# A two-layer GLA and S5 trunk: GpSimd's elementwise work goes to VectorE

## The chip, the cores and the metric

The kernel runs on one core of a Trainium2 chip. Its time is the device time of one execution in microseconds; the figure used is the median of three runs. Engines are TensorE (PE in the profile, its weight loads PEld), VectorE (DVE), ScalarE (ACT), GpSimd (POOL) and SyncE (SP, which here only issues DMAs).

## The reference

512 tokens of width 1024 pass two layers, each `x <- x + Mixer(RMSNorm(x))`, and a last RMSNorm. The first mixer is chunked gated linear attention (GLA) with 4 heads; the second is a grouped complex-diagonal state-space layer (S5) with 128 groups of 16 channels and 64 states each:

```
lam_bar = exp(lam * dt);  b_bar = (lam_bar - 1) / lam * b
states  = scan(states * lam_bar + b_bar u)
y = Re(c states) + d u;   y = gelu(y);   y = y * sigmoid(y w_glu + b_glu) * silu(z)
```

Everything is float32. All inputs arrive at run time, the S5 parameters too, so the matrices with which the S5 layer is computed are made in the kernel.

## The kernel before

**Dense products.** Every weight matrix comes in units of 128x1024 floats. `wunit` (L178) loads a unit into `wraw` (two buffers), lets ScalarE round it to a high half (`whl`, L161) and makes the low half, raw minus high, with `split` (L159, the subtraction is L162). `three` (L196) then does three matmuls per product. With `dma=True` (w_v of heads 1 to 3, w_z, w_qk) the low half is made by a DMA instead: ScalarE writes minus the raw unit (L186) and a DMA from GpSimd's queue adds the raw unit (L187). With `pool=True` (the S5 projections u and z and the first block of w_glu, 40 units) a list of zeros and ones, `UNITP`, says whether GpSimd or VectorE subtracts; 23 units go to GpSimd.

**The GLA layer** runs head by head. `weave` (L544) steps through the dense generators of a head and calls between the steps the parts of its attention (`scores`, `state`, `mix`) and, through `hook` (L369), the next steps of the S5 preparation, at a rate per phase (`RATES`).

**The S5 preparation** (class `S5Prep`). `small` (L971) makes the parameter tables, in good part on GpSimd (L993). Then for each of 16 blocks of 8 groups: `load` (L1271) fetches four tiles, `compute` (L1285) makes the products L1293 to L1311 on GpSimd, step F of the next block adds z and z2 on VectorE (`finish_b`, L1323) and stores the input matrix in two halves (`store`, L1317 on ScalarE, L1318 on VectorE), and step Z (`finish_z`, L1326) stores the output matrix, multiplies it with bh on TensorE (L1333) and makes from that the direct kernel (L1337 on ScalarE, L1339 on VectorE, L1342 to L1345 on GpSimd) and stores it. Step E (`etab`, L1250) makes one of eight tables of rotations with six products, on VectorE for the first `EV = 3` and on GpSimd for the others. Results go to DRAM and are fetched back by the S5 layer.

**The S5 layer.** For each block: `sT` transposes u, `sA` (L795) multiplies it with the input matrix, rotates, scans (L810), and rotates back: L812 on GpSimd, L813 to L815 on VectorE. `sB` (L817) makes halves of the state (L822, L823) and the output; `sC` the gelu; `s5` (L843) the product with the gate (L847, GpSimd) and the halves for the GLU.

**Order.** Each engine runs its instructions in one order, which a planner fixes ahead from priorities. `LOWS` puts the steps F, Z, E and G so far behind the work around them in priority. Each engine's queue, SyncE's DMA queue too, is worked through in that order. GpSimd also issues the adding DMAs (L187) and makes the powers of the RMS norms (L270).

Of the kernel before, what the change touches and what calls it, by code (L numbers as in the profile page):

```python
# [21 lines left out]
P = 128  # L22
# [33 lines left out]
TS = [2, 3, 3, 3, 4, 5, 5, 5, 6, 6, 7, 8, 10, 10, 11, 12]  # L56
ORDER = ['u0', 'u1', 'u2', 'z0', 'u3', 'z1', 'z2', 'z3', 'g0']
LOW1, LOW2 = 20, 0
EV = 3
SCP = -20  # L60
USP = 50
SEQ0 = 'h0 u h2 u h4 u s h6 u x0 t x1 q0 q1 t'
GP = 4
RATES = [0.84, 0.84, 0.88, 0.94, 0.94]
LOWS = {'F': 0, 'Z': 20, 'E': 100, 'G': 0}
ETABS = [2, 3, 3, 3, 3, 3, 3, 3, 4, 4, 4, 4, 4, 4, 4, 7, 8]
POS = [[0, 0, 1, 2, 1, 2, 3, 1, 2, 3, 3], [0, 1, 1, 3, 4, 5, 6, 5, 5, 7, 9], [0, 1, 3, 4, 4, 5, 6, 5, 6, 8, 8], [1,
    1, 4, 4, 4, 5, 6, 6, 6, 6, 8], [0, 0, 0, 0]]
# [5 lines left out]
SGS = [16, 16, 16, 16, 16, 16, 16, 16, 16, 16, 16, 17, 18, 19, 20, 21]  # L74
LAS = [0, 0, 0, 5, 6, 7, 8, 9, 10, 10, 11, 12, 13, 14, 15, 16]
LBS = [0, 0, 0, 6, 7, 7, 8, 9, 10, 11, 12, 13, 14, 15, 16, 18]
UNITP = [0, 1, 0, 1, 1, 1, 0, 1, 1, 1, 0, 1, 1, 0, 1, 1, 1, 1, 1, 0, 0, 1, 1, 1, 1, 1, 0, 1, 0, 0, 1, 0, 0, 0, 0, 0,
    0, 0, 1, 1]
TORD = ['c0 c1 s0 c2 x0 s1 x1 c3 s2 x2 x3', 'c0 c1 c2 c3 x0 s0 s1 x1 s2 x2 x3', 'c0 c1 c2 c3 s0 x0 s1 s2 x1 x2 x3',
    'c0 c1 c2 c3 s0 s1 x0 x1 s2 x2 x3']  # L80
PACE = [2, 2, 2, 2, 2, 2, 3, 1, 2, 2, 2, 2, 2, 2, 2, 2, 2, 2, 1, 1, 1, 1]
# [4 lines left out]
def f(t):  # L86
    return t.bitcast(F32) if t.dtype == F32R else t
# [3 lines left out]
def trunk_kernel(  # L91
# [5 lines left out]
    nc = tc.nc  # L97
# [58 lines left out]

    mark = {}

    def split(dst_hi, dst_lo, src, scale=None, E=V):  # L159
        if scale is None:  # L160
            i0 = A.copy(out=dst_hi, in_=src)  # L161
            i1 = E.tensor_tensor(out=dst_lo, in0=src, in1=f(dst_hi), op=SUB)  # L162
        else:
            i0 = A.activation(out=dst_hi, in_=src, func=AF.Copy, scale=scale)
            i1 = V.scalar_tensor_tensor(out=dst_lo, in0=src, scalar=scale, in1=f(dst_hi), op0=MUL, op1=SUB)  # L165
        return i0.ins, i1.ins
# [6 lines left out]
            V.tensor_scalar(out=dst_hi, in0=src, scalar1=scale, scalar2=None, op0=MUL)  # L173
            V.scalar_tensor_tensor(out=dst_lo, in0=src, scalar=scale, in1=f(dst_hi), op0=MUL, op1=SUB)

    wcnt = [0]

    def wunit(src, nk, ncol, pool=False, dma=False):  # L178
        raw = T_([P, nk, ncol], "wraw", WR)
        mark["sp"] = S.dma_start(out=raw.rearrange("p k n -> p (k n)"), in_=src).ins  # L180
        hi = T_([P, nk, ncol], "whl", WH, F32R)
        lo = T_([P, nk, ncol], "whl", WH, F32R)
        if dma:
            fl = "p k n -> p (k n)"
            A.copy(out=hi, in_=raw)  # L185
            mark["act"] = A.activation(out=lo, in_=raw, func=AF.Copy, scale=-1.0).ins  # L186
            G.dma_start(out=lo.rearrange(fl), in_=src, accum_op=ADD)  # L187
        else:
            E = V
            if pool:  # L190
                E = G if UNITP[wcnt[0]] else V
                wcnt[0] += 1
            mark["act"], mark["dve"] = split(hi, lo, raw, E=E)
        return hi, lo

    def three(acc, wh, wl, ah, al, first, last, weights_stationary):  # L196
# [6 lines left out]
            PE.matmul(acc, lhsT=ah, rhs=wl, start=False, stop=False)  # L203
            mark["pe"] = PE.matmul(acc, lhsT=al, rhs=wh, start=False, stop=last).ins  # L204

    def dense_tok(w, ah, al, evac, per_tb=False, late=True, major=1, pool=False, banks=None, dma=False):
        nkb = 4 if per_tb else len(ah)
        accs = [b() for b in banks or [PD] * NT]
        nu = nkb // 2

        def part(u, tb, hi, lo):
            for k in range(2):
                kb = 2 * u + k
                if per_tb:
                    cs = slice(kb * P, (kb + 1) * P)
                    xh, xl = ah[tb][:, cs], al[tb][:, cs]
                else:
                    cs = slice(tb * P, (tb + 1) * P)
                    xh, xl = ah[kb][:, cs], al[kb][:, cs]
                three(accs[tb], hi[:, k, :], lo[:, k, :], xh, xl, kb == 0, kb == nkb - 1, False)  # L220

        def fetch(u):
            return wunit(w[u], 2, 512, pool=pool, dma=dma)
        for u in range(nu - major + 1):
            if u == nu - major:
                ws = [fetch(v) for v in range(u, nu)]
                for tb in range(NT):
                    for i, (hi, lo) in enumerate(ws):
                        part(u + i, tb, hi, lo)
                    if major > 1:  # L230
                        evac(tb, accs[tb])
                if major > 1:
                    yield
                    return
            else:
                hi, lo = fetch(u)
                for tb in range(NT):
                    part(u, tb, hi, lo)
            if u == nkb // 2 - 1:
                if late:  # L240
                    yield
                for tb in range(NT):
                    evac(tb, accs[tb])
            if not (late and u == nkb // 2 - 1):
                yield

    def dense_ch(w, ah, al, evac, pool=False, banks=None):
        nkb = len(ah)
        accs = [b() for b in banks or [PD] * 4]
        for u in range(nkb // 2):  # L250
            hi, lo = wunit(w[u], 2, 512, pool)
            for m in range(4):
                for k in range(2):
                    kb = 2 * u + k
                    three(accs[m], hi[:, k, m * P:(m + 1) * P], lo[:, k, m * P:(m + 1) * P],
                          ah[kb], al[kb], kb == 0, kb == nkb - 1, True)
            if u == nkb // 2 - 1:
                for m in range(4):
                    evac(m, accs[m])
            yield  # L260
# [494 lines left out]
    def ev_z(cb, acc):  # L755
        zt = tmp()
        V.tensor_tensor(out=zt, in0=acc, in1=rb2, op=MUL)
        th = tmp()
        A.activation(out=th, in_=zt, func=AF.Tanh, scale=0.5)
        if cb < 12:  # L760
            z = big()
        else:
            if not z3:
                z3.append(T_([P, 4, 512], "u8", 1))
            z = z3[0][:, cb - 12]
        sz[cb] = z
        V.scalar_tensor_tensor(out=z, in0=th, scalar=1.0, in1=zt, op0=ADD, op1=MUL)
# [27 lines left out]
    def sA(cb):  # L795
        t = st_[cb]
        bm, uh = t["bm"], t["uh"]
        co, sn = t["cs"]
        r = rz[cb % 2]
        pv = PO()  # L800
        for g in range(GB):
            three16(pv, bm, g, uh[:, 0], uh[:, 1], True, True)
        t2 = tmp()
        V.tensor_tensor(out=t2[0:64], in0=pv[64:128, :], in1=sn[64:128, :], op=MUL)
        V.scalar_tensor_tensor(out=t2[64:128], in0=pv[0:64, :], scalar=-1.0, in1=sn[0:64, :], op0=MUL, op1=MUL)
        t1 = t["t1"] = tmp()
        V.tensor_tensor(out=t1, in0=pv, in1=co, op=MUL)
        V.tensor_tensor(out=t1, in0=t1, in1=t2, op=ADD)
        sh = xx()
        V.tensor_tensor_scan(out=sh, data0=r.rearrange("p g c -> p (g c)"), data1=t1, initial=0.0,  # L810
                             op0=MUL, op1=ADD)
        G.tensor_tensor(out=t1, in0=sh, in1=co, op=MUL)  # L812
        V.scalar_tensor_tensor(out=t2[0:64], in0=sh[64:128], scalar=-1.0, in1=sn[64:128], op0=MUL, op1=MUL)  # L813
        V.tensor_tensor(out=t2[64:128], in0=sh[0:64], in1=sn[0:64], op=MUL)
        V.tensor_tensor(out=t1, in0=t1, in1=t2, op=ADD)  # L815
# [27 lines left out]
    def s5(cb):  # L843
        if yh2[cb // 8] is None:
            yh2[cb // 8] = act2()
        yh[cb] = yh2[cb // 8][:, cb % 8, :]
        G.tensor_tensor(out=sz[cb], in0=sz[cb], in1=yv[cb], op=MUL)  # L847
        yl[cb] = xx(F32R) if cb == 0 else big(F32R)
        split(yh[cb], yl[cb], yv[cb])
        yv[cb] = None  # L850
# [12 lines left out]
    def win():  # L863
        for c in ORDER:
            n = int(c[1])
            if c[0] == "u":
                yield from dense_tok(s_wu[n], h2, l2, lambda tb, acc, n=n: ev_u(n, tb, acc), late=False, pool=True)
            elif c[0] == "z":
                yield from dense_ch(s_wz[n], h2, l2, lambda m, acc, n=n: ev_z(4 * n + m, acc), pool=True)
            else:  # L870
                yield from dense_ch(w_glu[n], yh, yl, lambda m, acc, n=n: ev_g(4 * n + m, acc), pool=True)

    jobs = {}

# [64 lines left out]
class S5Prep:  # L939
# [309 lines left out]

    def etab(self, ck):  # L1250
        nc = self.nc
        tt = (nc.vector if ck < EV else nc.gpsimd).tensor_tensor
        gs = slice(ck * GB, (ck + 1) * GB)
        hr, hi, lr, li = (t[:, gs] for t in self.et)
        shp = [P, GB, 8, 8]
# [27 lines left out]
        self.ld[cb] = (lp, bb, xc, pp)  # L1283

    def compute(self, cb):  # L1285
        G = self.nc.gpsimd
        tt = G.tensor_tensor
        lp, bb, xc, pp = self.ld.pop(cb)
        gs = slice(cb * GB, (cb + 1) * GB)
        v = lambda t: t.rearrange("p (g r q) -> p g r q", g=GB, r=2)  # L1290
# [35 lines left out]
    def finish_z(self, cb):  # L1326
# [10 lines left out]
        A.activation(out=ke, in_=pk[:, 0:P], func=AF.Copy, scale=self.par[:, 0:1])  # L1337
        kf = self.C2([P, P, 2], "kf", F16)
        V.scalar_tensor_tensor(out=ke, in0=pk[:, P:2 * P], scalar=self.par[:, 1:2], in1=ke, op0=MUL, op1=ADD)  # L1339
        G = nc.gpsimd  # L1340
        dk = self.C2([P, 16], "dk")
        G.tensor_tensor(out=dk, in0=self.dm, in1=self.kd[:, cb:cb + 1].to_broadcast([P, 16]), op=MUL)  # L1342
        G.tensor_tensor(out=ke[:, 0:16], in0=ke[:, 0:16], in1=dk, op=ADD)
        G.tensor_copy(out=kf[:, :, 0], in_=ke)
        G.tensor_tensor(out=kf[:, :, 1], in0=ke, in1=kf[:, :, 0], op=SUB)  # L1345
        S.dma_start(out=self.kz[cb * GB:(cb + 1) * GB, :, 224:480].rearrange("g i w -> (g i) w"),
                    in_=kf.rearrange("p w k -> p (w k)"))

# [81 lines left out]
```

## Time and profile before

| | us |
|---|---|
| three runs | 1053.78, 1055.71, 1055.98 |
| median | 1055.71 |
| the profiled execution | 1054.56 |
| its span in the profile | 1052.9 |

| engine | busy us | share of the span |
|---|---|---|
| PE | 927.6 | 88% |
| DVE | 713.8 | 68% |
| POOL | 511.0 | 49% |
| ACT | 472.2 | 45% |

A busy time is the time in which at least one instruction of that engine was under way; it includes time in which the instruction stood still. The rows that the prediction rests on stand below. In groups of instructions, a row gives line, engine, operation, output<-inputs, shapes and count, then busy time and mean length, then the idle time before them and what ended it.

### The profile page before, as it was taken

To read this page: it belongs to the slowest core of one execution; us is meant where nothing else is said; L and a number is where in the kernel's file an instruction comes from. 1 tells how busy PE (TensorE), PEld (TensorE's weight loads), DVE (VectorE), ACT (ScalarE), POOL (GpSimd) and SP (SyncE) were. 2 spreads that over 40 slices of the span, in tenths; PEclk is the share of its full clock that TensorE was granted. 3 is DMA by queue.
4 is the path that set the end of the run, shared out by engine and by line. 5 is a ranking of instruction groups with operands and counts; after the bars stand their busy time and mean duration, and the time that the engine had idled before them with its cause. 6 is when DMAs were issued, how large, how long until landed. Compare 5 with 4: busy or idle time off the path is not lost. (4 is left out here: it accounts for less than half of the span.)

```text
span 1052.9 us, 13715 instructions
## 1 busy us (share of the span) xinstructions
PE 927.6 (88%) x5019; PEld 720.8 (68%) x5019; DVE 713.8 (68%) x916; ACT 472.2 (45%) x707; POOL 511.0 (49%) x477
## 2 busy tenths in 40 slices
PE   6795966699869796969989999999998999999996
PEld 5573754457646684747777777787777888888885
DVE  5794569957898887978645769789897432424322
ACT  5553343445546455433556684744453332313222
POOL 4164808976897979899973434453314000000000
PEclk9897987999889998989999999999999999999998
DMA  8884466999969899999578447687854323353312
GB/s 256 221 183 100 87 167 185 276 247 262 265 209 250 228 292 273 237 321 317 190 226 259 151 121 250 211 300 252 264 185 140 110 82 99 100 160 100 100 61 80
DMA packets 118707, 205.79 MB, mean 195 GB/s; under 512 B 32400, under 2 KB 69824, under 8 KB 118640
## 3 DMA queue, kind: packets, MB, share of 16 engines
q1 hardware_dynamic: 110208, 180.90, 55.2%
q0 software_dynamic: 5472, 19.02, 10.0%
q10 hardware_dynamic: 2960, 4.99, 1.3%
q8 instruction: 39, 0.64, 0.3%
q14 instruction: 28, 0.23, 0.1%
HBM read 167.69 MB, written 45.59 MB: 203 GB/s over the span
## 5 line engine op out<-in xcount | busy, mean ns | idle before, releaser
L162 DVE TENSOR_TENSOR whl<-wraw,whl 128x1024 fp32r<-128x1024 f32 x77 | 106.6, 1384 | 147.5 <-ACT whl L161 147.3
L161 ACT CAST whl<-wraw 128x1024 fp32r<-128x1024 f32 x100 | 104.7, 1048 | 183.7 <-PE pt L199 46.0
L202 PE MATMUL pd<-whl,actA 128*128 128x512 f32 x384 | 154.6, 408 | 12.9 <-ACT whl L161 9.2
L203 PE MATMUL pd<-whl,actA 128*128 128x512 f32 x384 | 154.2, 402 | 0.0
L204 PE MATMUL pd<-whl,actA 128*128 128x512 f32 x384 | 154.0, 404 | 0.0
L270 POOL TENSOR_TENSOR rstd<-rv,neghalf 128x1 f32<-128x1 f32 (+1 forms) x6 | 5.2, 874 | 248.4 <-DVE rv L269 248.4
L198 PE MATMUL pd<-actA,whl 128*128 128x512 f32 x256 | 101.6, 403 | 3.3 <-ACT u L732 3.1
L200 PE MATMUL pd<-actA,whl 128*128 128x512 f32 x256 | 101.4, 397 | 0.0
L202 PEld LDWEIGHTS pd<-whl,actA 128*128 128x128 f32 x384 | 74.4, 194 | 32.7 <-ACT whl L161 9.2
L202 PE MATMUL pd<-whl,q 128*128 128x512 f32 x192 | 80.3, 419 | 11.7 <-DVE xx L541 5.1
L204 PEld LDWEIGHTS pd<-whl,actA 128*128 128x128 f32 x384 | 73.9, 193 | 18.6 <-issue 2.8
L203 PEld LDWEIGHTS pd<-whl,actA 128*128 128x128 f32 x384 | 73.9, 192 | 17.7 <-issue 2.1
L162 POOL TENSOR_TENSOR whl<-wraw,whl 128x1024 fp32r<-128x1024 f32 x23 | 58.3, 2533 | 52.5 <-ACT whl L161 49.2
L203 PE MATMUL pd<-whl,q 128*128 128x512 f32 x192 | 79.6, 415 | 0.0
L1318 DVE TENSOR_TENSOR q<-q,q 128x1024 f16<-128x1024 f32 x32 | 60.4, 1886 | 12.6 <-ACT q L1317 12.3
L198 PEld LDWEIGHTS pd<-actA,whl 128*128 128x128 f32 x256 | 48.5, 190 | 16.6 <-ACT u L732 5.2
L1293 POOL TENSOR_TENSOR q<-q,q 128x1024 f32<-128x1024 f32 x16 | 43.4, 2709 | 31.7 <-DMA q<-s_bi 29.6
L198 PE MATMUL po<-actA,whl 128*128 128x512 f32 x128 | 52.4, 409 | 5.8 <-ACT whl L185 5.8
L185 ACT CAST whl<-wraw 128x1024 fp32r<-128x1024 f32 x36 | 37.7, 1046 | 44.0 <-PE pd L203 26.4
L200 PEld LDWEIGHTS pd<-actA,whl 128*128 128x128 f32 x256 | 48.4, 189 | 11.2
L204 PE MATMUL pd<-whl,q 128*128 128x512 f32 x128 | 53.7, 424 | 1.4 <-DVE q L165 1.4
L202 PEld LDWEIGHTS pd<-whl,q 128*128 128x128 f32 x192 | 38.4, 200 | 23.6 <-DVE xx L541 6.4
(334 smaller groups left out, 2484.4 us busy)
## 6 DMA issues: line engine op xcount, KB each, us to landing
wraw<-w_glu SPq DMA_DIRECT2D x32, 512.0 KB, 3.4
wraw<-w_v SPq DMA_DIRECT2D x16, 512.0 KB, 5.4
wraw<-w_z SPq DMA_DIRECT2D x16, 512.0 KB, 6.5
whl<-w_z POOLq DMA_DIRECT2D x16, 512.0 KB, 7.9
wraw<-w_out SPq DMA_DIRECT2D x16, 512.0 KB, 6.8
q<-lpt SPq DMA_DIRECT2D x16, 512.0 KB, 6.8
q<-s_bi SPq DMA_DIRECT2D x16, 512.0 KB, 9.5
tab<-q SPq DMA_DIRECT2D x32, 256.0 KB, 4.2
```

What stands on the lines that cost most here:

```text
L161: i0 = A.copy(out=dst_hi, in_=src)
L162: i1 = E.tensor_tensor(out=dst_lo, in0=src, in1=f(dst_hi), op=SUB)
L185: A.copy(out=hi, in_=raw)
L198: PE.matmul(acc, lhsT=wh, rhs=ah, start=first, stop=False)
L200: mark["pe"] = PE.matmul(acc, lhsT=wl, rhs=ah, start=False, stop=last).ins
L202: PE.matmul(acc, lhsT=ah, rhs=wh, start=first, stop=False)
L203: PE.matmul(acc, lhsT=ah, rhs=wl, start=False, stop=False)
L204: mark["pe"] = PE.matmul(acc, lhsT=al, rhs=wh, start=False, stop=last).ins
L270: G.tensor_tensor(out=dst, in0=v, in1=neghalf.to_broadcast([P, w]), op=ALU.pow)
L1293: tt(out=m, in0=lp, in1=bb, op=MUL)
L1318: nc.vector.tensor_tensor(out=hl[:, 1], in0=src, in1=hl[:, 0], op=SUB)
```

## The change

All products of `compute` and `etab`, the four small operations at the end of `finish_z`, the low halves that `UNITP` gave to GpSimd, L812 and L847 are issued on VectorE. The settings of two steps in `LOWS` change from 0 and 20 to 30. GpSimd keeps the adding DMAs, the powers and the products of `small`.

```diff
-EV = 3
...
-LOWS = {'F': 0, 'Z': 20, 'E': 100, 'G': 0}
+LOWS = {'F': 30, 'Z': 30, 'E': 100, 'G': 0}
...
-UNITP = [0, 1, 0, 1, 1, 1, 0, 1, 1, 1, 0, 1, 1, 0, 1, 1, 1, 1, 1, 0, 0, 1, 1, 1, 1, 1, 0, 1, 0, 0, 1, 0, 0, 0, 0, 0,
-    0, 0, 1, 1]
...
-    def split(dst_hi, dst_lo, src, scale=None, E=V):
+    def split(dst_hi, dst_lo, src, scale=None):
         if scale is None:
             i0 = A.copy(out=dst_hi, in_=src)
-            i1 = E.tensor_tensor(out=dst_lo, in0=src, in1=f(dst_hi), op=SUB)
+            i1 = V.tensor_tensor(out=dst_lo, in0=src, in1=f(dst_hi), op=SUB)
...
-            E = V
-            if pool:
-                E = G if UNITP[wcnt[0]] else V
-                wcnt[0] += 1
-            mark["act"], mark["dve"] = split(hi, lo, raw, E=E)
+            mark["act"], mark["dve"] = split(hi, lo, raw)
...
-        G.tensor_tensor(out=t1, in0=sh, in1=co, op=MUL)
+        V.tensor_tensor(out=t1, in0=sh, in1=co, op=MUL)
...
-        G.tensor_tensor(out=sz[cb], in0=sz[cb], in1=yv[cb], op=MUL)
+        V.tensor_tensor(out=sz[cb], in0=sz[cb], in1=yv[cb], op=MUL)
...
     def etab(self, ck):
         nc = self.nc
-        tt = (nc.vector if ck < EV else nc.gpsimd).tensor_tensor
+        tt = nc.vector.tensor_tensor
...
     def compute(self, cb):
-        G = self.nc.gpsimd
-        tt = G.tensor_tensor
+        tt = self.nc.vector.tensor_tensor
...
-        G = nc.gpsimd
         dk = self.C2([P, 16], "dk")
-        G.tensor_tensor(out=dk, in0=self.dm, in1=self.kd[:, cb:cb + 1].to_broadcast([P, 16]), op=MUL)
-        G.tensor_tensor(out=ke[:, 0:16], in0=ke[:, 0:16], in1=dk, op=ADD)
-        G.tensor_copy(out=kf[:, :, 0], in_=ke)
-        G.tensor_tensor(out=kf[:, :, 1], in0=ke, in1=kf[:, :, 0], op=SUB)
+        V.tensor_tensor(out=dk, in0=self.dm, in1=self.kd[:, cb:cb + 1].to_broadcast([P, 16]), op=MUL)
+        V.tensor_tensor(out=ke[:, 0:16], in0=ke[:, 0:16], in1=dk, op=ADD)
+        V.tensor_copy(out=kf[:, :, 0], in_=ke)
+        V.tensor_tensor(out=kf[:, :, 1], in0=ke, in1=kf[:, :, 0], op=SUB)
```

The parameter `pool` of `wunit`, `dense_tok` and `dense_ch` goes with it.

## Rows read from the trace of the kernel before

**Rows 1.** The page: its first line.

```profile
span 1052.9 us, 13715 instructions
```

**Rows 2.** Busy time by stretch; the last columns are granted clock, DMA share, GB/s.

```profile
150.00:550.00 400.00, 329.21 (x1413) 245.39 (x1413) 322.00 (x333) 187.53 (x296) 336.51 (x285) 0.90 0.88 253
550.00:650.00 100.00, 96.72 (x801) 76.64 (x800) 69.53 (x93) 65.21 (x87) 40.59 (x27) 0.99 0.61 196
650.00:800.00 150.00, 137.80 (x1198) 111.66 (x1198) 134.93 (x158) 72.53 (x105) 56.41 (x39) 0.98 0.72 233
```

**Rows 3.** Waits of TensorE, 150 to 550 us: total, times, longest, in us.

```profile
PE po L202 <- ACT big L164: 14.5, 2, 11.1
PE pt L1333 <- DVE q L1323: 12.3, 2, 6.5
PE pt L1333 <- POOL bh L1311: 7.6, 2, 5.4
```

**Rows 4.** Timeline, 352 to 368 us: start and length in us.

```profile
352.92 7.34 DVE L535 TENSOR_TENSOR rsv<-rsv,rstd 128x4 f32<-128x4 f32 x1 [1.34 <-POOL rsv L270]
...
360.18 7.09 DVE L1323 TENSOR_TENSOR q<-q,q 128x1024 f32<-128x1024 f32 x1
```

**Rows 5.** Timeline of VectorE, 174 to 180 us.

```profile
175.41 1.21 DVE L162 TENSOR_TENSOR whl<-wraw,whl 128x1024 fp32r<-128x1024 f32 x1
176.54 1.21 DVE L1318 TENSOR_TENSOR q<-q,q 128x1024 f16<-128x1024 f32 x1
177.68 1.21 DVE L1323 TENSOR_TENSOR q<-q,q 128x1024 f32<-128x1024 f32 x1
```

**Rows 6.** VectorE's groups, 825 to 1035 us: busy us, mean ns, idle before.

```profile
L162 DVE TENSOR_TENSOR whl<-wraw,whl 128x1024 fp32r<-128x1024 f32 x36 | 44.1, 1225 | 124.2 <-ACT whl L161 124.2
...
L925 DVE TENSOR_TENSOR actA<-actA,q 128x512 f32<-128x512 f32 x4 | 2.7, 684 | 0.1
```

**Rows 7.** VectorE's groups, 150 to 550 us.

```profile
L1318 DVE TENSOR_TENSOR q<-q,q 128x1024 f16<-128x1024 f32 x32 | 60.4, 1886 | 12.6 <-ACT q L1317 12.3
L162 DVE TENSOR_TENSOR whl<-wraw,whl 128x1024 fp32r<-128x1024 f32 x18 | 33.4, 1857 | 11.2 <-ACT whl L161 11.2
L1323 DVE TENSOR_TENSOR q<-q,q 128x1024 f32<-128x1024 f32 x16 | 30.2, 1891 | 0.0
L398 DVE SCALAR_TENSOR_TENSOR big<-tmp,rsv,big 128x512 f32<-128x512 f32 x12 | 24.1, 2038 | 0.0
...
L174 DVE SCALAR_TENSOR_TENSOR big<-big,ges,big 128x512 fp32r<-128x512 f32 x9 | 18.5, 2052 | 0.1
...
L173 DVE TENSOR_SCALAR big<-big,ges 128x512 fp32r<-128x512 f32 x9 | 13.5, 1498 | 0.1
L535 DVE TENSOR_TENSOR rsv<-rsv,rstd 128x4 f32<-128x4 f32 x3 | 11.2, 3749 | 3.1 <-POOL rsv L270 3.1
...
L165 DVE SCALAR_TENSOR_TENSOR big<-pd,rstd,big 128x512 fp32r<-128x512 f32 x12 | 8.7, 739 | 0.5 <-ACT big L164 0.5
...
L162 DVE TENSOR_TENSOR big<-pt,big 128x128 fp32r<-128x128 f32 x8 | 2.2, 279 | 0.0
```

**Rows 8.** GpSimd's groups, 150 to 550 us, same columns.

```profile
L1293 POOL TENSOR_TENSOR q<-q,q 128x1024 f32<-128x1024 f32 x16 | 43.4, 2709 | 31.7 <-DMA q<-s_bi 29.6 <-issue 1.7 <-DMA tab<-q 0.4
...
L1296 POOL TENSOR_TENSOR q<-q,q 128x512 f32<-128x512 f32 x16 | 28.6, 1789 | 0.0
...
L1311 POOL TENSOR_TENSOR bh<-bh,bh 128x128 f32<-128x128 f32 x16 | 14.7, 920 | 0.1
```

**Rows 9.** GpSimd's groups, whole span.

```profile
L162 POOL TENSOR_TENSOR whl<-wraw,whl 128x1024 fp32r<-128x1024 f32 x23 | 58.3, 2533 | 52.5 <-ACT whl L161 49.2 <-issue 3.3
...
L812 POOL TENSOR_TENSOR tmp<-xx,q 128x512 f32<-128x512 f32 x13 | 22.4, 1722 | 46.9 <-DVE xx L810 30.2 <-issue 16.7
```

**Rows 10.** VectorE's groups, 550 to 800 us.

```profile
L814 DVE TENSOR_TENSOR tmp<-xx,q 64x512 f32<-64x512 f32 x12 | 19.3, 1604 | 0.2
...
L823 DVE SCALAR_TENSOR_TENSOR q<-tmp,q 128x504 f16<-128x504 f32 x15 | 17.2, 1144 | 2.6 <-ACT q L822 2.3
```

More of the change, by code (lines that the diff above doesn't have):

```diff
@@ L174, in split1, with wunit @@
             V.scalar_tensor_tensor(out=dst_lo, in0=src, scalar=scale, in1=f(dst_hi), op0=MUL, op1=SUB)
-    wcnt = [0]
-    def wunit(src, nk, ncol, pool=False, dma=False):
+    def wunit(src, nk, ncol, dma=False):
         raw = T_([P, nk, ncol], "wraw", WR)
@@ L204, in three, with dense_tok @@
             mark["pe"] = PE.matmul(acc, lhsT=al, rhs=wh, start=False, stop=last).ins
-    def dense_tok(w, ah, al, evac, per_tb=False, late=True, major=1, pool=False, banks=None, dma=False):
+    def dense_tok(w, ah, al, evac, per_tb=False, late=True, major=1, banks=None, dma=False):
         nkb = 4 if per_tb else len(ah)
@@ L222, in fetch @@
         def fetch(u):
-            return wunit(w[u], 2, 512, pool=pool, dma=dma)
+            return wunit(w[u], 2, 512, dma=dma)
         for u in range(nu - major + 1):
@@ L245, in dense_tok, with dense_ch @@
                 yield
-    def dense_ch(w, ah, al, evac, pool=False, banks=None):
+    def dense_ch(w, ah, al, evac, banks=None):
         nkb = len(ah)
@@ L250, in dense_ch @@
         for u in range(nkb // 2):
-            hi, lo = wunit(w[u], 2, 512, pool)
+            hi, lo = wunit(w[u], 2, 512)
             for m in range(4):
@@ L866, in win @@
             if c[0] == "u":
-                yield from dense_tok(s_wu[n], h2, l2, lambda tb, acc, n=n: ev_u(n, tb, acc), late=False, pool=True)
+                yield from dense_tok(s_wu[n], h2, l2, lambda tb, acc, n=n: ev_u(n, tb, acc), late=False)
             elif c[0] == "z":
-                yield from dense_ch(s_wz[n], h2, l2, lambda m, acc, n=n: ev_z(4 * n + m, acc), pool=True)
+                yield from dense_ch(s_wz[n], h2, l2, lambda m, acc, n=n: ev_z(4 * n + m, acc))
             else:
-                yield from dense_ch(w_glu[n], yh, yl, lambda m, acc, n=n: ev_g(4 * n + m, acc), pool=True)
+                yield from dense_ch(w_glu[n], yh, yl, lambda m, acc, n=n: ev_g(4 * n + m, acc))
     jobs = {}
```

## The prediction

> **What bounds the kernel now.** I read the page first, then the busy time by stretches, then TensorE's waits inside the stretch that loses most, then the instructions behind those waits.
>
> The profiled execution took 1054.56 us, with a span of 1052.9 [rows 1]; it stands 1.15 us under the median of the three runs, 1055.71, and all sums below are made against 1054.6. About 0.2% (2 us) is what a measurement of this kernel can tell from no change.
>
> The stretches [rows 2] show where time can go. From 150 to 550 us, where the GLA heads run and the S5 preparation (steps F, Z, E) is woven between them, TensorE is busy for 329.2 of 400 us and its granted clock is 0.90, between the two levels of 1.2 and 2.4 GHz. No single engine is full there: VectorE 322.0, GpSimd 336.5, ScalarE 187.5, the DMA engines 0.88. From 550 to 650 and from 650 to 800, where the S5 layer is computed, TensorE is at 96.7 of 100 and 137.8 of 150. The last 250 us hold next to none of the moved work. So the first of these stretches is the one to argue about: 71 us of TensorE idle.
>
> Among TensorE's waits in it [rows 3], 12.3 us in two waits are for the sum z+z2 (L1323, VectorE) ahead of the small matmuls of finish_z (L1333), and 7.6 us in two waits are for the same matmuls' other operand, bh (L1311, GpSimd). The largest pair, 14.5 us, ends with ScalarE's high half of v (L164).
>
> The timeline [rows 4] shows why L1323 is late. An operation on four elements per partition (L535) stands on VectorE for 7.34 us and L1323 for 7.09 us right behind it, while GpSimd runs one product after another. On the same engine L1323 also takes 1.21 us [rows 5]. VectorE is not computing in those 14 us, it is held up: its busy time is part work and part standing still.
>
> **What is moved, and its price on VectorE.** Clean prices are read where GpSimd does nothing [rows 6]: 1225 ns for 128x1024 and 684 ns for 128x512. For 128x128 it is 279 ns, with an input in PSUM [rows 7]. Successive operations start 1.13 us apart though each is 1.21 us long [rows 5], so each takes 0.08 us less of the engine than its length.
>
> Per step F/Z, 16 times (one group of each of the larger shapes is in [rows 8]): three products of 128x1024 (L1293, L1302, L1304), four of 128x512 (L1294 to L1297), five of 128x128 (L1309 to L1311, L1344, L1345) and two of 128x16, which I also price at 279 as an upper bound, their lower bound being the overlap of 0.08. That is 3 x 1.225 + 4 x 0.684 + 7 x 0.279 = 8.36 us, less 14 x 0.08 = 7.24 us, and 116 us for the 16. GpSimd's own price is 2709, 1789 and 920 ns for these shapes. The E tables from the fourth on: five of them with six operations each, 30 x (0.684 - 0.08) = 18 us. Together 134 us more for VectorE from 150 to 550.
>
> In the S5 stretches [rows 9]: 23 low halves of 128x1024 (I put all of them there), 23 x 1.145 = 26 us; 16 state products L812 and 16 gate products L847 of 128x512, 32 x 0.604 = 19 us. Together 46 us. GpSimd takes 2533 and 1722 ns for the two shapes.
>
> **What VectorE gets back.** In the first stretch these groups [rows 7] are longer than the clean price: L1318 by 32 x (1886 - 1225) = 21 us, L162 by 18 x (1857 - 1225) = 11, L1323 by 16 x (1891 - 1225) = 11, L398 by 12 x (2038 - 739) = 16, L174 by 9 x (2052 - 739) = 12, L173 by 9 x (1498 - 684) = 7, L535 by 3 x (3749 - 279) = 10 (with the price of the larger 128x128). The clean price of a scalar_tensor_tensor, 739, is L165's in the same rows, whose input lies in PSUM and which isn't stretched. Sum 88 us, in groups that hold 191 of the 322 us. The other 131 us are not all clean either; at half that rate they give another 30 us, an estimate. The rows alone leave 322 - 88 + 134 = 368 us of 400; with the estimate 338. In the S5 stretches L814 gives back 12 x (1604 - 684) = 11 us and L823 15 x (1144 - 684) = 7 [rows 10], so 204.5 + 46 - 18 = 232 of 250.
>
> So VectorE's load comes out near what it shows today, a little above, while most of GpSimd's 336 us fall away. What is left on GpSimd reads little: the accumulating DMAs (L187), the powers (L270) and the parameter products ahead of 150 us, which stay and keep their price.
>
> **Queues that the steps pass.** GpSimd's queue holds L187 behind the moved products today; afterwards those DMAs wait for ScalarE's negated copy alone. I count nothing for it, since other units lie ahead in the buffers; its bounds are 0 and the idle time of TensorE that no row here names, 71 - 34 = 37 us of gain. SyncE's queue is in order: the loads of the next block (L1278 to L1282) wait until compute has released its tiles, and the stores (L1319, L1346) until the sums are ready, so a late product on VectorE holds back weight loads behind it. It moves no DMA, only the time at which its release comes; cost between 0 and the rival below. The settings 30 for F and Z (from 0 and 20) put these products behind the layer's own hand-offs in the planner's order. That costs nothing while the next load of a block lies ahead; if the cover is gone, L1333 is late next, and TensorE stands in order behind it.
>
> **The sum.** I take from the first stretch the two waits at L1333, 12.3 + 7.6 = 19.9 us, which a held-up operation and a GpSimd operation end. A higher granted clock and the shorter L398 and L174 would add to it, new queueing on VectorE would take from it; I let these cancel. The bounds are 0 to 48 us of gain (the stretch cannot be shorter than its DMA work, 0.88 x 400 = 352), and the loss below. 380 us then hold 338 us of VectorE work, 89%, about the 134.9 of 150 (90%) that it shows today from 650 to 800. In the S5 stretches TensorE is at 94%, and I take 0: shorter L812 and L814 against 28 us more load. 1054.6 - 20 = 1034.6, or **1035 us**.
>
> **Rivals.**
> - *The preparation no longer holds anything up.* All of TensorE's waits on VectorE shrink, the clock stays up, and DMA sets the stretch: 1054.6 - 48 = 1007 us. For it: three of the waits in the first stretch alone make 34 of 71 us. Against: the DMA share would have to go to 1.0 with no gap.
> - *VectorE's queue becomes the bound* (the side of slower). One in-order queue now carries the preparation and the hand-offs to TensorE (L541, L396, L165). Place: 150 to 550 us first, then 650 to 800. Price: if the load is 368 us and VectorE fills 88%, the stretch takes 418 us, 18 more; 232 us at 90% take 258 instead of 250, 8 more. 1054.6 + 26 = 1081 us. It decides from the point where VectorE's share stays under load over 400, that is 92% with 368 us and 85% with 338; today it is 80.5%, though at a mixture with a second full engine. For it: 80.5%, and the static order. Against: the gaps of today lie around held-up operations. The Trainium skill speaks for this rival ("Perfetto Trace Analysis", Optimizing Scalar/DVE Operations): where VectorE is saturated, giving work to ScalarE or even GpSimd may make sense, so taking it back would not; the same passage warns that the two share an SBUF read port, so that such a move may not help. The 7.34 us of L535 agree with the warning.
> - *Nothing moves*: loads and stores set the pace at a DMA share of 0.88 whichever engine makes the products, 1055 us. Against: few of TensorE's waits in these rows end with a transfer.
>
> **Chances.** The forecast has 0.42 (1020 to 1050), DMA-bound 0.20, VectorE's queue 0.30, nothing 0.08. Faster by over 0.2%: 0.42 + 0.20 = 0.62, less 0.01 for its edge near zero, 0.61. Within 0.2%: 0.08, less what falls to either side, 0.07. Slower: 0.32. The range reaches from 1005, which leaves out somewhat under half of the first rival (0.08), to 1085, which leaves out a third of the second (0.10), the part in which the S5 stretches lose more than the 8 us counted.
>
> **What would show it.** Right: no DVE group from 150 to 550 us over 1.3 us for 128x1024 (L1318 and L1323 at 1.2), L535 under 0.5 us, GpSimd busy under 60 us there, VectorE between 330 and 370, the two waits at L1333 under 3 us each, the stretch some 20 us shorter. Wrong: TensorE's waits for DVE L541, L165 or L396 sum to over 40 us, VectorE has no gaps and the stretch is longer; or DVE stays stretched beside the DMAs' issues (L187); or the time is lost from 550 to 800, where L823 and L787 would be late for TensorE.

## The result, and the profile after

The changed kernel takes 1044.47 us (median of four runs, 1042.20 to 1045.83) against 1055.85 us of the kernel before in the same runs: a ratio of 0.9894, with a 95% interval of 0.9859 to 0.9928. The forecast was 1035 us, a gain of 20; about 11 us came. The profiled execution took 1042.20 us, its span is 1040.5. Ratios leave out runs over 1.5% above the fastest of their kernel, which matters most for e4_idle_products, where it is two of six.

Lines in the changed kernel have other numbers, since the diff takes lines out: L1318 of before is L1308, L1323 is L1313, L1333 is L1323, L396 is L387, L398 is L389, L535 is L526, L541 is L532, L162 is L159, L165 is L162, L173 is L170, L174 is L171, L187 is L182, L493 (the scores) is L484, L408 (the transposes of o) is L399.

Busy time by stretch (PE, PEld, DVE, ACT, POOL, then granted clock, DMA share, GB/s), to set beside [rows 2]:

```profile
150.00:550.00 400.00, 333.24 (x1472) 251.13 (x1473) 329.84 (x602) 198.48 (x313) 28.88 (x33) 0.89 0.89 261
550.00:650.00 100.00, 91.92 (x768) 73.55 (x767) 74.88 (x114) 58.27 (x81) 0.51 (x3) 0.97 0.49 164
650.00:800.00 150.00, 144.45 (x1255) 114.81 (x1254) 133.39 (x188) 73.70 (x106) 1.73 (x10) 1.00 0.72 235
```

GpSimd is down from 336.5 to 28.9 us in the first stretch, and VectorE, which does that work now, is only 7.8 us above what it showed before. TensorE begins 1472 matmuls there in place of 1413, at about the same clock (0.89 in place of 0.90).

VectorE's groups from 150 to 550 us (busy us, mean ns, idle before), to set beside [rows 7]:

```profile
L1308 DVE TENSOR_TENSOR q<-q,q 128x1024 f16<-128x1024 f32 x32 | 38.8, 1217 | 0.4 <-ACT q L1307 0.3
L159 DVE TENSOR_TENSOR whl<-wraw,whl 128x1024 fp32r<-128x1024 f32 x24 | 29.1, 1217 | 15.0 <-ACT whl L158 15.0
...
L1313 DVE TENSOR_TENSOR q<-q,q 128x1024 f32<-128x1024 f32 x16 | 19.5, 1216 | 0.0
...
L389 DVE SCALAR_TENSOR_TENSOR big<-tmp,rsv,big 128x512 f32<-128x512 f32 x12 | 8.6, 741 | 0.0
...
L171 DVE SCALAR_TENSOR_TENSOR big<-big,ges,big 128x512 fp32r<-128x512 f32 x9 | 6.7, 741 | 0.0
...
L170 DVE TENSOR_SCALAR big<-big,ges 128x512 fp32r<-128x512 f32 x9 | 4.3, 478 | 0.0
...
L526 DVE TENSOR_TENSOR rsv<-rsv,rstd 128x4 f32<-128x4 f32 x3 | 0.5, 153 | 0.9 <-POOL rsv L261 0.9
```

Every one is at its clean length or near it: the low halves of the stored matrices, L1308, at 1217 ns (before 1886), L1313 at 1216 (1891), L389 at 741 (2038), L171 at 741 (2052), L170 at 478 (1498), and the operation on four elements, L526, at 153 ns (3749).

TensorE's waits in the same stretch (total, times, longest), to set beside [rows 3]:

```profile
PE pt L484 <- DVE big L159: 18.1, 2, 14.2
PE pt L1323 <- DVE q L162: 8.4, 2, 7.5
PE pt L399 <- DVE q L162: 8.2, 3, 6.8
PE pt L484 <- DVE tmp L1329: 7.0, 2, 5.7
PE pt L1323 <- DVE big L159: 6.5, 2, 5.7
PE pt L484 <- DVE q L162: 5.4, 3, 2.6
PE pd L193 <- DVE tmp L387: 4.6, 2, 2.7
PE po L193 <- ACT big L161: 3.7, 1, 3.7
```

No wait for z+z2 or for bh is left, and the 14.5 us for v's high half have become 3.7. In their place stand waits for VectorE's hand-offs. The longest, 14.2 us at one place, is a score matmul (L484) waiting for VectorE's low half of transposed keys (L159 in the form big<-pt,big), which is read from the kind of PSUM tile that L484 writes; meanwhile VectorE works without a gap through the products of the first preparation steps, and TensorE does nothing:

```profile
157.87:172.07 14.20, 0.01 (x1) 0.00 (x0) 14.20 (x23) 3.78 (x6) 0.00 (x0) 0.50 0.53 173
```

Where the gain appears can be read by counting TensorE's 3416 matmuls with 512 columns in both traces. On the way the changed kernel is not ahead all the time: the 450th starts 19.3 us later than before (191.4 against 172.1), amid the crowd of the first steps, the 750th 2.8 us earlier, the 1350th 2.7 us later again (463.4 against 460.7). By then the moved products of all 16 blocks have been started, and nothing is gained. The 1500th starts 5.9 us earlier and the 1650th 13.5 us (552.1 against 565.6); the 2400th is 13.2 earlier (793.4 against 806.6), the last one 12.4. So the gain comes in two short stretches: the last dense products of the GLA layer (1350th to 1500th) and the first projections of the S5 layer (1500th to 1650th). Columns as above, first before, then after:

```profile
460.69:514.14 53.45, 43.80 (x197) 33.18 (x196) 46.01 (x53) 23.55 (x44) 52.80 (x37) 0.90 0.93 303
514.14:565.59 51.45, 46.49 (x245) 37.04 (x243) 20.56 (x30) 28.61 (x43) 36.55 (x33) 0.93 0.69 207
```

```profile
463.37:508.23 44.86, 41.65 (x190) 31.93 (x188) 39.02 (x78) 20.41 (x40) 1.03 (x1) 0.96 0.78 267
508.23:552.06 43.83, 41.18 (x206) 32.50 (x206) 25.16 (x46) 26.28 (x40) 3.02 (x6) 1.00 0.75 231
```

In the first of the two, TensorE is idle for 3.2 us in place of 9.7; the wait of 6.5 us for z+z2 [rows 3] lay there. In the second it is idle for 2.7 us in place of 5.0 and busy for 5.3 us less, at a granted clock of 1.00 in place of 0.93; before, GpSimd made the last tables and the first low halves there. The trace of e6_after_again, the same kernel, repeats this: 3.6 us behind at the 1350th, 5.4 ahead at the 1500th, 13.0 at the 1650th.

### The profile page after: what moved, and what is told of

Same layout as the page of the kernel before. It is cut to its first block, busy times and chain, and to the rows that moved or that the text cites. A ratio compares the mean times of both kernels' runs of the same rounds, so it can differ in the third digit from the quotient of the medians.

```text
span 1040.5 us, 13590 instructions
## 1 busy us (share of the span) xinstructions
PE 921.3 (89%) x5019; PEld 715.9 (69%) x5019; DVE 715.5 (69%) x1225; ACT 471.4 (45%) x707; POOL 101.2 (10%) x168
## 5 line engine op out<-in xcount | busy, mean ns | idle before, releaser
L159 DVE TENSOR_TENSOR whl<-wraw,whl 128x1024 fp32r<-128x1024 f32 x100 | 122.0, 1222 | 156.5 <-ACT whl L158 156.2
L193 PE MATMUL pd<-whl,actA 128*128 128x512 f32 x384 | 152.9, 404 | 13.3 <-ACT whl L158 9.0
L194 PE MATMUL pd<-whl,actA 128*128 128x512 f32 x384 | 153.0, 398 | 0.0
L195 PE MATMUL pd<-whl,actA 128*128 128x512 f32 x384 | 151.4, 399 | 0.0
L189 PE MATMUL pd<-actA,whl 128*128 128x512 f32 x256 | 102.3, 406 | 7.3 <-ACT u L723 6.2
L191 PE MATMUL pd<-actA,whl 128*128 128x512 f32 x256 | 101.4, 397 | 0.0
L193 PEld LDWEIGHTS pd<-whl,actA 128*128 128x128 f32 x384 | 73.1, 191 | 32.4 <-ACT whl L158 9.0
L195 PEld LDWEIGHTS pd<-whl,actA 128*128 128x128 f32 x384 | 72.9, 190 | 17.6 <-issue 2.4
L194 PEld LDWEIGHTS pd<-whl,actA 128*128 128x128 f32 x384 | 73.1, 190 | 16.9 <-issue 1.2
L193 PE MATMUL pd<-whl,q 128*128 128x512 f32 x192 | 79.0, 412 | 4.4 <-DVE tmp L387 2.7
L194 PE MATMUL pd<-whl,q 128*128 128x512 f32 x192 | 77.9, 406 | 0.0
L189 PE MATMUL po<-actA,whl 128*128 128x512 f32 x128 | 51.7, 404 | 3.8 <-ACT whl L180 3.8
L190 PE MATMUL pd<-actA,whl 128*128 128x512 f32 x128 | 52.1, 407 | 0.0
L191 PE MATMUL po<-actA,whl 128*128 128x512 f32 x128 | 50.4, 396 | 1.3 <-DMA whl<-w_qk 1.3
L195 PE MATMUL pd<-whl,q 128*128 128x512 f32 x128 | 50.9, 409 | 0.0
L723 ACT ACTIVATE u<-pd,rsP 64x256 f32<-64x256 f32 x64 | 48.2, 753 | 3.5 <-DVE mxr L716 2.6
L190 PE MATMUL pd<-big,whl 128*128 128x512 f32 x120 | 47.6, 398 | 1.1 <-DVE big L159 1.1
```

The source lines that it names most:

```text
L159: i1 = V.tensor_tensor(out=dst_lo, in0=src, in1=f(dst_hi), op=SUB)
L189: PE.matmul(acc, lhsT=wh, rhs=ah, start=first, stop=False)
L190: PE.matmul(acc, lhsT=wh, rhs=al, start=False, stop=False)
L191: mark["pe"] = PE.matmul(acc, lhsT=wl, rhs=ah, start=False, stop=last).ins
L193: PE.matmul(acc, lhsT=ah, rhs=wh, start=first, stop=False)
L723: A.activation(out=dst, in_=src, func=AF.Copy, scale=rsP[hs, tb:tb + 1])
```

## The experiments

Three theories were set against each other. **H** (hold): VectorE's operations are held up while GpSimd makes products, and the gain is the end of that. **L** (latency): the products are simply ready sooner on the faster engine. **P** (plan): the gain is the new order that the planner makes from the new settings. **Q**, formed after the first runs: VectorE's one queue is the new wait. All ratios are against the kernel before in the same measurement; single runs of one kernel spread widely (the kernel before in one measurement: 1046.3 to 1060.4), so a difference of a few us between two kernels is only told from their intervals.

**e6_after_again.** The changed kernel unedited, measured a second time:

> The changed kernel once more, unaltered, in five rounds on one chip with the others. H, L and P alike: a ratio of 0.986 to 0.993, and TensorE's waits from 150 to 550 us at VectorE's hand-offs again near 60 us.

Measured: 1045.67 us, ratio 0.9907 (0.9872 to 0.9943), and TensorE's waits again with the same head:

```profile
PE pt L484 <- DVE big L159: 18.1, 2, 14.2
PE pt L1323 <- DVE q L162: 8.7, 2, 8.1
```

The waits for VectorE from 150 to 550 us sum to 63 us, near the 60 expected. So a gain of 0.9 to 1.1% stands, and the waits for VectorE's hand-offs belong to the program and are no accident of one execution.

**e1_old_priorities.** The changed kernel, with

```diff
-LOWS = {'F': 30, 'Z': 30, 'E': 100, 'G': 0}
+LOWS = {'F': 0, 'Z': 20, 'E': 100, 'G': 0}
```

> The changed kernel with the two settings of LOWS put back (F 0, Z 20). Theory H: the gain comes from VectorE's operations no longer being held up by GpSimd's products; the settings add little, so 1042 to 1050 us. Theory L: the gain comes from the preparation's products being done sooner by a faster engine; the same range. Theory P: the gain comes from the new priorities, that is from the planner's order; then 1051 to 1058.

Measured: 1046.98 us, ratio 0.9961 (0.9935 to 0.9987). The time lies in the range of H and L and not in P's: the move alone makes the kernel faster. The ratio, though, lies between before and after (0.9961 against 0.9894 and 0.9907; its interval lies clear of the first of these two and overlaps the second), as if the settings were worth about half of the gain. The trace does not put that where the settings act. By the 1650th counted matmul e1 is 15.7 us ahead of the kernel before, more than the 13.5 of the changed kernel; it loses half of that lead in the S5 layer, where no step F or Z is left, at a lower granted clock (first e1, then the changed kernel):

```profile
750.00:800.00 50.00, 43.23 (x334) 34.31 (x335) 44.95 (x63) 23.52 (x37) 0.00 (x0) 0.86 0.68 214
```

```profile
750.00:800.00 50.00, 46.63 (x405) 37.12 (x404) 47.51 (x66) 24.79 (x38) 0.18 (x1) 1.00 0.68 212
```

So whether P has a part in the gain is not settled.

**e2_prep_alone and e3_s5_alone.** The kernel before with one half of the change each; e2 has the new settings, e3 the old ones:

```diff
 e2: compute, etab, the end of finish_z and the two settings
-LOWS = {'F': 0, 'Z': 20, 'E': 100, 'G': 0}
+LOWS = {'F': 30, 'Z': 30, 'E': 100, 'G': 0}
...
-        tt = G.tensor_tensor
+        tt = self.nc.vector.tensor_tensor
...
 e3: the low halves, L812 and L847
-                E = G if UNITP[wcnt[0]] else V
+                E = V
...
```

> The kernel before with only the preparation moved to VectorE (compute, etab, the end of finish_z, and the two settings); the 23 low halves, L812 and L847 stay on GpSimd. H and L: three quarters or more of the gain, 1043 to 1049 us, with the means of L1318 and L1323 under 1.35 us. If the gain lies in the S5 part instead: 1053 to 1058.

> The kernel before with only the S5 part moved to VectorE (the 23 low halves, L812, L847); the preparation stays on GpSimd, settings as before. H: L814 falls from 1.6 to 0.7 us, but TensorE is at 94% there, so a small gain, 1050 to 1056 us; L1318 stays at 1.7 to 2.0 us. If the S5 part carries the gain: 1043 to 1048.

Measured: e2 1052.45 us, ratio 0.9990 (0.9968 to 1.0011); e3 1049.75 us, ratio 0.9979 (0.9955 to 1.0003). The first rows are VectorE's groups of e2 from 150 to 550 us, the second those of e3:

```profile
L1317 DVE TENSOR_TENSOR q<-q,q 128x1024 f16<-128x1024 f32 x32 | 38.9, 1219 | 0.2 <-ACT q L1316 0.2
...
L1322 DVE TENSOR_TENSOR q<-q,q 128x1024 f32<-128x1024 f32 x16 | 19.5, 1218 | 0.0
```

```profile
L1318 DVE TENSOR_TENSOR q<-q,q 128x1024 f16<-128x1024 f32 x32 | 64.8, 2026 | 10.7 <-ACT q L1317 10.6
...
L1323 DVE TENSOR_TENSOR q<-q,q 128x1024 f32<-128x1024 f32 x16 | 30.9, 1933 | 1.6 <-POOL q L1304 1.6
```

The lengths came as expected: clean where GpSimd makes no preparation products, 2026 and 1933 ns where it does. The times did not; neither lies in a range that was given for it. The preparation alone, which clears all of these operations, gains nothing that can be told from zero, though three quarters of the gain were expected. The halves' gains, 0.1% and 0.2%, do not add up to the whole. The traces look otherwise. There e2 is 6.3 us ahead of the kernel before at the 1500th counted matmul, like the changed kernel, and e3 gains its 7.0 us between the 1500th and the 1650th, where the changed kernel gains 7.6; at the end they are 6.8 and 5.8 us ahead, together about the 12.4 of the whole. But e2's profiled execution, 1047.98 us, is the shortest of its twelve, so single executions and medians disagree here, and why is open.

**e4_idle_products and e5_idle_memsets.** The changed kernel, and GpSimd does extra work per step F whose result nobody reads, once products and once memsets:

```diff
         self.res[cb] = (bo, z, z2, bh)
...
+        for _ in range(24):
+            self.nc.gpsimd.tensor_tensor(out=self.dum, in0=self.ident, in1=self.ident, op=MUL)
 or
+        for _ in range(80):
+            self.nc.gpsimd.memset(self.dum, 0.0)
```

> The changed kernel, and GpSimd also makes 24 products of 128x128 per step F (384 in all, some 0.6 us each, 230 us in all) into a tile that nobody reads. H: VectorE's operations are held up again (means of L1318 and L1323 over 1.5 us) and the time goes back by half or more, 1050 to 1062 us. L: nothing waits for these products, so within 4 us of the changed kernel, 1041 to 1048.

> The changed kernel, and GpSimd also does 80 memsets of 128x128 per step F (about 0.2 us each, 16 us per step, as long as the 24 products of e4_idle_products) into a tile that nobody reads. They keep GpSimd's queue as full but read nothing. If the 72 us of e4_idle_products came from VectorE and GpSimd holding each other up: within 10 us of the changed kernel, 1040 to 1055. If they came from the queue, where the adding DMAs (L182) stand behind the extra work: 1090 us or more.

Measured: the products 1116.52 us (median of six runs, 1106.27 to 1134.41; the trace is of the longest), ratio 1.0557 (1.0514 to 1.0600); the memsets 1047.97 us, ratio 0.9942 (0.9917 to 0.9966). GpSimd's groups over the whole span, first with products, then with memsets:

```profile
L1306 POOL TENSOR_TENSOR dum<-ident 128x128 f32<-128x128 f32 x384 | 265.7, 692 | 24.4
L182 POOL DMA_DIRECT2D whl<-w_z x16 | 14.0, 892 | 59.3 <-DVE big L171 26.5 <-ACT whl L181 26.0 <-DVE q L162 6.5
```

```profile
L1306 POOL MEMSET dum<- 128x128 f32 x1280 | 280.9, 219 | 68.6
L182 POOL DMA_DIRECT2D whl<-w_z x16 | 13.8, 864 | 24.7 <-ACT whl L181 19.1 <-ACT q L161 4.2 <-issue 0.6
```

The two fill GpSimd for about as long, 265.7 and 280.9 us, with the same adding DMAs (L182) in its queue. The memsets hold nothing up. With them GpSimd is busy for 243.8 of the 400 us from 150 to 550, L1312 (L1318 of before) is at its clean length, and the time is 2.3 us over e6's, with intervals that overlap:

```profile
150.00:550.00 400.00, 328.40 (x1461) 247.32 (x1462) 327.95 (x600) 196.62 (x313) 243.77 (x1072) 0.89 0.87 256
L1312 DVE TENSOR_TENSOR q<-q,q 128x1024 f16<-128x1024 f32 x32 | 38.8, 1216 | 3.0 <-ACT q L1311 3.0
```

The products cost some 65 us more by the ratios, and both theories had missed that size. Not all of it can be put down to their reading SBUF. The planner set both kinds of extra work among the parameter products of small, one behind every operation or two there, where a product takes more of GpSimd's queue than a memset. With the products the last of L984 starts at 155.5 us and the preparation's first product (L1283) at 189.7 us, with the memsets at 122.8 and 148.5, in the changed kernel at 122.0 and 151.8. A late preparation is thus part of the cost, and how large a part is not shown. The holds are shown by lengths, but not those that H named: L1312 was 1279 ns on average, not over 1500. They went elsewhere. The low halves of the weights from 100 to 200 us, with products and with memsets:

```profile
L159 DVE TENSOR_TENSOR whl<-wraw,whl 128x1024 fp32r<-128x1024 f32 x4 | 19.4, 4874 | 8.6 <-ACT whl L158 8.6
```

```profile
L159 DVE TENSOR_TENSOR whl<-wraw,whl 128x1024 fp32r<-128x1024 f32 x4 | 5.3, 1314 | 1.8 <-ACT whl L158 1.8
```

One of the four with products lasted 15.6 us. And the planner had put GpSimd's products between the adding DMAs: TensorE's waits from 150 to 550 us of the run with products begin with one for those DMAs, which the changed kernel does not have:

```profile
PE pd L194 <- DMA whl<-w_z: 15.9, 3, 13.3
```

GpSimd's idle products, all of one shape, last from 0.39 to 3.45 us. That fits GpSimd being held up in its turn; no run tests it by itself.

**e7_s5_idle_products.** The same with 8 products of 128x256 in each step sA:

```diff
...
+        for _ in range(8):
+            G.tensor_tensor(out=dum.rearrange("p (a b) -> p a b", a=2), in0=ident.unsqueeze(1).to_broadcast([P, 2, P]),
+                            in1=ident.unsqueeze(1).to_broadcast([P, 2, P]), op=MUL)
         pv = PO()
```

> The changed kernel, and in each of the 16 sA steps GpSimd makes 8 products of 128x256 (about 7 us, as long as what it did there before) into a tile that nobody reads; no adding DMA is in its queue in these stretches. H: VectorE's groups with two inputs in SBUF (L804 to L806, L814, the low halves L159) are longer by 15% or more and the time goes up by 4 to 12 us over the changed kernel. L: no one waits for them, so within 2 us.

Measured: 1094.38 us, ratio 1.0371 (1.0330 to 1.0412), and as a test of the S5 stretches it failed. The products wait for nothing, so the planner put all 128 of them ahead of 250 us, among the parameter products of small. There they show the hold at its plainest (timeline of VectorE and GpSimd; start and length in us):

```profile
147.21 25.26 DVE L159 TENSOR_TENSOR whl<-wraw,whl 128x1024 fp32r<-128x1024 f32 x1 [5.55 <-ACT whl L158]
...
147.34 0.82 POOL L794 TENSOR_TENSOR dum<-ident 128x256 f16<-128x256 f32 x1
...
147.91 0.73 POOL L990 TENSOR_TENSOR big<-q,q 128x128 f32<-128x128 f32 x1
...
148.40 0.81 POOL L794 TENSOR_TENSOR dum<-ident 128x256 f16<-128x256 f32 x1
```

One low half of a weight unit, 1.2 us of work, lasts 25.26 us, while GpSimd goes from product to product, none of them longer than 1.5 us. The busy time around it (columns as above):

```profile
150.00:172.00 22.00, 13.67 (x64) 11.07 (x63) 22.00 (x1) 1.05 (x1) 21.92 (x31) 0.92 0.14 44
172.00:180.00 8.00, 0.00 (x0) 0.00 (x0) 3.53 (x4) 2.09 (x2) 7.37 (x9) 0.50 0.52 157
```

From 150 to 172 us VectorE has this one instruction in 22 us, GpSimd 31. The next weight load waits for it (19.5 us in SyncE's queue), ScalarE waits 19.1 us for that load, and TensorE does nothing from 172 to 180. The extra products also stand in front of the parameter products here: the preparation's first product starts at 204.3 us in place of 151.8, so the whole cost is again not that of the holds alone.

**e8_low_priority.**

```diff
-LOWS = {'F': 30, 'Z': 30, 'E': 100, 'G': 0}
+LOWS = {'F': 80, 'Z': 80, 'E': 100, 'G': 0}
```

> The changed kernel with both settings at 80 in place of 30: the preparation's products stand further behind the hand-offs in VectorE's order. If TensorE's remaining waits are the hand-offs queued behind these products (L159 and L162 at L484, L399, L1323): 1030 to 1040 us. If the order is not what sets them, or the matmuls of finish_z come too late then: 1044 to 1060.

Measured: 1063.77 us, ratio 1.0085 (1.0051 to 1.0119), slower than before and beyond both ranges. Putting the preparation further back does not shorten the hand-offs' waits, the wait at L484 for L159 stays at 18.1 us in two waits, and those at L1323 and L387 grow:

```profile
PE pt L484 <- DVE big L159: 18.1, 2, 14.2
PE pt L1323 <- DVE q L162: 15.3, 2, 8.7
PE pd L193 <- DVE tmp L387: 10.9, 2, 7.2
```

With e1 this makes three places of the same products in VectorE's order: 0.9961, 0.9894 and 0.9907, and 1.0085.

**e9_tables_later and e11_steps_spread.** Two ways to thin out the crowd on VectorE at the head starts:

```diff
 e9
-ETABS = [2, 3, 3, 3, 3, 3, 3, 3, 4, 4, 4, 4, 4, 4, 4, 7, 8]
+ETABS = [0, 0, 0, 1, 1, 2, 2, 3, 4, 4, 4, 4, 4, 4, 4, 7, 8]
 e11
-RATES = [0.84, 0.84, 0.88, 0.94, 0.94]
+RATES = [0.9, 0.9, 0.94, 1.0, 1.0]
-QZ = [2, 3]
+QZ = [1, 3]
```

> The changed kernel with the first three steps E (the rotation tables) due three to seven blocks later, so that they no longer stand with the first steps F in VectorE's order from 150 to 190 us. Q (VectorE's queue is the new wait there): TensorE's wait at L484 for VectorE's L159, 18.1 us in the changed kernel, falls by 5 us or more, and the time by 3 to 8 us, to 1036 to 1042. If the crowd does not set the time (the dense units are made up later anyway): 1043 to 1048 whatever the wait does.

> The changed kernel with one step of the preparation in place of two at the head of each GLA head (QZ), and the rates of the others raised by 6%, so that the same steps are spread more evenly. Q: TensorE's waits at L484 and L399 from 100 to 250 us fall and the time is 1036 to 1043 us. If the steps' place does not matter: 1043 to 1048.

Measured: e9 1050.96 us, ratio 0.9974 (0.9948 to 1.0000); e11 1059.88 us, ratio 1.0057 (1.0031 to 1.0083); both lie over both of their ranges. TensorE's waits of e9 from 50 to 250 us:

```profile
PE pt L484 <- DVE q L162: 9.0, 1, 9.0
...
PE pt L484 <- DVE big L159: 5.7, 1, 5.7
```

The wait for L159 fell from 18.1 to 5.7 us and one of 9.0 us for another hand-off came up at the same matmuls. By the 600th of the counted matmuls e9 is ahead of the changed kernel, at 220.0 us against 228.4; by the 1500th it is behind, at 513.1 against 508.2. So a shorter stall at one head start did not reach the end: what e9 gained there it lost again later, with the tables in later places. Which of the later waits did that is not settled.

**e10_parameters_too.** The changed kernel, and the products of small on VectorE too:

```diff
-        def tt(o, a, b, op, E=G):
+        def tt(o, a, b, op, E=V):
...
-        def ts(o, a, s1, op0, s2=0.0, op1=ADD, E=G):
+        def ts(o, a, s1, op0, s2=0.0, op1=ADD, E=V):
```

(and three copies).

> The changed kernel with the parameter products of small (L984, L987 and three copies) on VectorE too, so that GpSimd is left with no elementwise work from 60 to 125 us but the powers. H: the VectorE operations that are still held up there (15 us over the shortest of their kind between 50 and 125 us) become clean and the preparation starts sooner, 1034 to 1043 us. Q: VectorE has more to do at the time when the first head's hand-offs need it, 1046 to 1056 us.

Measured: 1035.61 us, ratio 0.9835 (0.9799 to 0.9871), the lowest time of all: its six runs (1032.22 to 1038.45) lie below all runs of both kernels, though its interval still overlaps that of the changed kernel's first measurement. The first rows are the changed kernel's, the second e10's (VectorE's groups from 50 to 125 us):

```profile
L999 DVE TENSOR_TENSOR big<-big 128x64 f32<-128x64 f32 x11 | 4.5, 427 | 0.1
L389 DVE SCALAR_TENSOR_TENSOR big<-tmp,rsv,big 128x512 f32<-128x512 f32 x4 | 4.4, 1135 | 0.0
```

```profile
L389 DVE SCALAR_TENSOR_TENSOR big<-tmp,rsv,big 128x512 f32<-128x512 f32 x4 | 2.9, 740 | 0.0
...
L999 DVE TENSOR_TENSOR big<-big 128x64 f32<-128x64 f32 x11 | 2.4, 224 | 0.0
```

What was still held up there is clean now, 740 in place of 1135 ns and 224 in place of 427. The 300th counted matmul starts 3.0 us earlier than in the changed kernel, the 600th 10.3 us, the last one 8.3 us; the preparation's first product starts at 143.3 us in place of 151.8. The time lies in H's range, 1034 to 1043. Since the parameter products are also shorter on VectorE (those of L984 with 128x512 685 ns, 1230 and more on GpSimd), this run does not separate H from L either.

**e12_attention_first.** e10 with one more setting:

```diff
-SCP = -20
+SCP = -60
```

> e10_parameters_too with the attention's parts (scores, state, mix) 60 in place of 20 ahead of the work around them in the planner's priority. Q: TensorE's waits at L484 for VectorE (14.6 and 8.8 and 5.2 us in e10_parameters_too) fall by half and the time by 4 to 10 us, to 1025 to 1032. If a shorter wait there only turns up at the next hand-off: 1033 to 1040.

Measured: 1038.66 us, ratio 0.9881 (0.9832 to 0.9929), no better than e10. The wait at L484 for L159 is 14.6 us as in e10, and the others there came to more:

```profile
PE pt L484 <- DVE big L159: 14.6, 1, 14.6
PE pt L484 <- DVE tmp L1329: 12.3, 3, 6.7
...
PE pt L484 <- DVE q L162: 7.7, 2, 7.5
```

A priority further ahead did not shorten these waits, and the time lies in the range given for that, 1033 to 1040.

## Why the prediction was right or wrong

**What bounds, and the hold: right.** The long operations on VectorE were standing still, not computing. All seven groups named fell to their clean length, L535 from 3749 to 153 ns; L173 fell to 478 ns, under the 684 taken as its clean price. In e5, memsets on GpSimd leave VectorE's operations clean; in e4 and e7, single operations last 15.6 and 25.26 us beside products. That the gain in time comes from the end of the holds alone is not shown: the change also makes the products themselves shorter, and no run separates the two.

**VectorE's load: right.** Forecast were 338 us with the estimate and 368 from the rows alone; it is 329.8. The estimate for the groups without rows was even somewhat low. Four of the 23 low halves, all counted for the S5 stretches, were made before 550 us (by GpSimd, starting from 511.9 to 534.3 us). So the work that GpSimd did in over 300 us costs VectorE next to nothing net, and the second rival's price, 368 us at 88%, did not come. GpSimd was forecast under 60 us and has 28.9.

**The S5 stretches: right from 550 us on.** Taken at 0; from the 1650th to the 2400th counted matmul it was 241.0 us before and 241.4 after, although L814 and L823 of [rows 10] fell to 685 and 677 ns. The Trainium skill ("Perfetto Trace Analysis", Optimizing Scalar/DVE Operations) says that offloading to GpSimd may make sense where VectorE is saturated. Here the measurement goes against that advice and with its own warning of the shared read port: with VectorE at 133.4 of 150 us from 650 to 800, the work came back at no loss. The S5 layer's first projections, just ahead of 550 us, gained 7.6 us, and for these the prediction had no term.

**The sum: the right mechanism, mis-sized.** The step that failed is the one that took the two waits at L1333, 19.9 us, and let new queueing on VectorE cancel with everything else. Those two waits are gone as waits for z+z2 and bh. But TensorE's idle time from 150 to 550 us went only from 70.8 to 66.8 us (400 - 333.2, with 59 matmuls more in the stretch), because the hand-offs now queue on VectorE: 18.1 + 7.0 + 5.4 us at the scores and 8.4 + 6.5 us even at the same small matmuls. TensorE's waits for VectorE other than those for z+z2 sum to 34 us there before and to 65 us after, with the smaller rows below those shown; its waits for ScalarE fell from 16 to 5. The term "new queueing" is therefore some 31 us and not something that cancels, and by the 1500th counted matmul 5.9 us were left of the 19.9. The 11.4 us at the end came as near to 20 as they did partly by luck, through the 7.6 us of the first S5 projections. Of the sign set for the second rival, over 40 us on L541, L165 and L396, 29.8 came (0.3 + 24.9 + 4.6); the longest stands at an operation not named, the low half of the transposed keys. That rival had the right place, and e8 and e11 lost more than the whole gain with the steps elsewhere in the order.

**The settings: no term of their own.** The prediction let them cost nothing while there is cover. With the old ones the ratio is 0.9961 and with the new ones about 0.990, but e1's trace does not place that difference in the preparation. With 80 it is 1.0085, and the wait at L1323 (L1333 of before) grows from 8.4 to 15.3 us, the place that the prediction named for cover that is gone.

**Left open.** Why the medians of the halves e2 and e3 gain so little is not settled. What bounds the stretch now is not settled either: e9, e11 and e12 shortened or moved single waits on VectorE and did not gain. One thing to try next was not tried: loads. VectorE itself waits 26.0 us for q<-s_bi in seven waits in the changed kernel, at a DMA share of 0.89, and the first rival's end of 1007 us assumed a share of 1.0.

## What to carry to other kernels

When a short operation on VectorE shows a mean far over its clean length, read what GpSimd is doing beside it: the time can be a hold, and the work that GpSimd does may be free on VectorE. Price VectorE's load after a move by its clean lengths minus the holds that end, not by busy shares. That gives the load and not yet the time, for the moved work queues in front of the hand-offs in VectorE's one order; in e8 a worse place there cost more than the move had gained (1.0085 against 0.9907 in the same measurement).

## What the runs showed of the hardware

A hold is not limited to one instruction of the other engine. The 25.26 us of e7 lasted through over 30 GpSimd instructions, the 7.34 and 7.09 us of [rows 4] through several. The Trainium skill ("SBUF — State Buffer", Who interferes with whom) says that an operation on VectorE with two inputs in SBUF contends with a GpSimd instruction that reads SBUF and not with one that only writes it. That agrees with the lengths in e4 (4874 ns for the low halves from 100 to 200 us) and e5 (1216 ns for L1312 beside memsets). The Trainium skill ("SBUF — State Buffer", SBUF: two separate sides) also says that the one that starts first has the shared ports for its whole instruction and the other blocks. Here the runs show more: a train of short reading instructions kept VectorE out far longer than any one of them. What at last lets it in, these rows do not tell.

VectorE's operation L165 with an input in PSUM was not held up in the first place: it had 739 ns in [rows 7] and has 741 ns now. An operation with one tile and a scalar per partition as inputs, L173, was held up: 1498 ns before, 478 now.
